# Low parts of the weights on VectorE, layer 1's value tile behind its four u tiles, and new durations in the kernel's own scheduler

## The chip, the cores and the metric

The kernel runs on one core of one Trainium2 chip. The metric is the device time of one execution in microseconds, lower is better. Five engines have instruction streams of their own: TensorE (PE in the profile, its weight loads PEld), VectorE (DVE), ScalarE (ACT), GpSimd (POOL) and SyncE (SP), which issues all DMA transfers. Each engine takes its stream strictly in order, and an instruction waits on semaphores for results of others; what stands behind a waiting instruction waits too.

## What is computed

Two layers of a diffusion backbone over 128 context tokens and 1024 latent tokens, model width 1024. Each layer, cut to what matters here:

```python
h = _rmsnorm(x, norm_w) * (1.0 + scale) + shift      # shift, scale, gate = split(silu(c) @ w_ada + b_ada)
p = h @ w_in                                          # (tokens, 2304): q 512, k 128, v 128, ga 512, u 512, gp 512
q, k = _rope_2d(q), _rope_2d(k)                       # latent tokens only
attn = banded attention, |i-j| <= 128, plus all 128 cached context keys, with a sink logit
pool = (window means of u, windows 2, 4, 8, 16, minus u) @ w_pool * pool_scale
a  = _rmsnorm(attn) * attn_norm * silu(ga);  pl = _rmsnorm(pool) * pool_norm * silu(gp)
x  = x + gate * (concatenate([a, pl]) @ w_out)
```

After the second layer comes one more rmsnorm. All of it is fp32. The new keys and values of the context tokens are outputs too.

## The kernel before

**Tiling.** Activations lie transposed, features on partitions. The 1152 tokens are three groups of 384 columns (group 0: 128 context and 256 latent tokens; buffers `G_81`, `G_82`, `G_83` hold x and later q and the pool result of groups 0, 1, 2). A projection *job* is one tile of 128 output features for one group: `project` issues 24 matmuls of 384 columns into one PSUM buffer `acc`, of which there are two. The 24 are 8 input blocks k times three, since an fp32 value is carried as a high and a low part of type fp32r: `w_hi*h_hi + w_hi*h_lo + w_lo*h_hi`. The parts of h are in `H_78`, `H_79`, `H_80` (groups 0, 1, 2); those of a weight tile in `wh`, of which there are two buffers.

**Weights.** `wload` fetches a weight tile in two halves of 128x512 into `wr` (or into slots of `R`). `wsplit` makes of each half the high part (a cast on ScalarE) and the low part (raw minus high). Which engine subtracts is one line:

```python
eng = self.V_ if i in self.WDVE or second is not None and h == 0 else self.P_
```

`WDVE = (0, 1, 2)` names the first three weight tiles; `second` marks the tiles of the second pass of the output projection, which loads the eight tiles again for group 2. All others are on GpSimd. A `wh` buffer comes free when its tile's last job is done, so the cast of tile n+2 waits for TensorE's last job of tile n.

**Stages of a layer.** 18 tiles times 3 groups are 54 jobs of the input projection, in the order of a list: u0, u1, v, u2, u3, k, q0 to q3, gp0 to gp3, ga0 to ga3; then 24 jobs of the output projection, 16 for groups 0 and 1, then 8 for group 2. With 78 jobs a layer there are 156. Beside them run: `pool_mix` (window sums of the u tiles in the buffer `R` on VectorE, small edge products on GpSimd, matmuls from `pth` and `ptl`), of which u2 and u3 need the buffers of u0 and u1 and after which the cosine and sine tables are loaded over `R` (`R<-in_cs`); the rotation of k and q, which needs these tables; `attention`, 18 units a layer (scores `pst<-K,qs` and `pst<-K,ql`, masked maximum into `s` on VectorE, exponentials on ScalarE, `den` on VectorE, normalisation `s<-s,den` on GpSimd, transposes `pst<-cst,s`, a split into `pth` on ScalarE and `ptl` on VectorE, products `pv<-..,V`); and at the layer's end `zsplit`, which overwrites `H` with the gated branches once the group's last job of the input projection is done. `next_h` then makes layer 1's `H` while the second pass runs.

**What sets the order.** Nothing is scheduled at run time. While the program is built, each stage is a Python generator, and `Sched.run` takes the step with the best priority among those whose estimated time has come; whatever it issues goes to the end of its engine's stream. The clock is TensorE's: `Tensor.issue` moves it on by an estimated cost, and the jobs (`main`, priority 9) fill in, three matmuls at a step, when nothing else is due. `Engine.cost` estimates the other engines, and `ready` adds `LAT` to a result that another engine made. So wrong estimates do not make a wrong result, they make another order. Before, one matmul of 384 columns is reckoned at 384/2.39 = 161 ns, every hand-over between engines at 190 ns, and VectorE and GpSimd as independent.

Of the kernel before, what the change touches and what calls it, by code (L numbers as in the profile page):

```python
# [84 lines left out]
class Engine:  # L85
# [7 lines left out]

    def cost(self, op, n, args, kw):
        if self.name == "act":
            return (205 if "accum_out" in kw else 107) + 0.763 * n
        if self.name == "dve":
            if op == "reciprocal":
                return 70 + 6.6 * n
            if op == "tensor_scalar" and not any(isinstance(x, bass.AP) and x.space == bass.MemoryType.PSUM for x in args):  # L100
                return 70 + 0.52 * n
            return 70 + 1.04 * n
        if op == "tensor_tensor" and kw.get("op") == ALU.pow:
            return 400 + 165 * n
        return 70 + {"tensor_tensor": 2.35, "scalar_tensor_tensor": 1.46}.get(op, 1.2) * n

    def __getattr__(self, op):
        f = getattr(self.eng, op)

        def call(*args, **kw):  # L110
# [6 lines left out]
            self.free = start + self.cost(op, free_size(args[0]), args, kw)  # L117
            s.commit(ins, outs, self.free, self.name)
            s.step_end = max(s.step_end, self.free + s.LAT)
# [4 lines left out]
class Tensor:  # L124
    def __init__(self, sched, eng):
        self.sched, self.eng = sched, eng

    def issue(self, ins, out, c):
        s = self.sched
        start = max(s.clock, s.ready(ins, [out], "pe"))  # L130
        s.stall += start - s.clock
        s.clock = start + c
        s.commit(ins, [out], s.clock + 60, "pe")
        s.step_end = max(s.step_end, s.clock + 60 + s.LAT)

    def matmul(self, out, lhsT, rhs, start, stop):
        self.eng.matmul(out, lhsT, rhs, start=start, stop=stop)  # L137
        n = free_size(rhs)
        if rhs.dtype == R32:
            c = n / 2.39 if n >= 256 else 213  # L140
        elif lhsT.shape[-1] > 32:
            c = max(n * 4 / 2.4, 426)
        else:
            c = n * 4 / 2.4 / 4
        self.issue([lhsT, rhs], out, c)

    def transpose(self, out, in_, ident):
        self.eng.transpose(out, in_, ident)  # L148
        self.issue([in_], out, 109)
# [19 lines left out]
class Sched:  # L169
# [3 lines left out]
    LAT = 190  # L173

    def __init__(self):
# [5 lines left out]
        self.mem = {}  # L181

    def ready(self, ins, outs, eng):
        t = 0.0
        for aps, write in ((ins, False), (outs, True)):
            for ap in aps:
                name, p0, p1, lo, hi = span(ap)
                for (q0, q1, l, h), e in self.mem.get(name, {}).items():
                    if q0 < p1 and p0 < q1 and l < hi and lo < h:
# [3 lines left out]
                        elif eng != "pe":  # L193
                            t = max(t, w)
# [57 lines left out]
class Kernel:  # L252
# [9 lines left out]
    WDVE = (0, 1, 2)  # L262
# [921 lines left out]
    def main(self, order):  # L1184
# [3 lines left out]
        for l in range(DEPTH):  # L1188
# [50 lines left out]
    def run(self):  # L1239
        a = self.a  # L1240
        order = [COL_U, COL_U + 1, COL_V, COL_U + 2, COL_U + 3, COL_K, 0, 1, 2, 3] + [COL_GP + j for j in range(4)] + [COL_GA + j for j in range(4)]
        items = []
        self.order, self.items = order, items
# [66 lines left out]
```

## Time and profile before

| | us |
|---|---|
| median of 3 runs (lowest to highest) | 972.14 (969.76 to 972.52) |
| the profiled execution | 972.32 |
| its span, first to last instruction | 970.5 |
| TensorE matmuls busy | 919.0 (95%) |
| VectorE busy | 710.6 (73%) |
| ScalarE busy | 533.1 (55%) |
| GpSimd busy | 404.2 (42%) |

The span is 1.8 us shorter than the profiled execution's own time. Busy means that at least one instruction of the engine was in progress. In the timeline views a bracket behind a row is the idle time of that engine just before the row and what ended it.

### The profile page before, as it was taken

The numbers are of one execution on the slowest core, as the hardware profiler recorded it, in microseconds if no ns is written. First come the engines' busy times: TensorE is split into PE (matmuls) and PEld (weight loads), VectorE is DVE, ScalarE is ACT, GpSimd is POOL, SyncE is SP. The second block draws the span as 40 slices with busy tenths as digits, with TensorE's granted clock in tenths as the row PEclk, the third lists the DMA queues.
The fourth block names the chain that finished last, engine by engine and source line by source line (L and its number), as shares of the span: only waits on it lengthen the run. The fifth ranks groups of instructions, "written<-read, shape, count | busy, mean of one in ns | idle before, by whom it ended". The sixth has DMA issues, their size and how long they took to land.

```text
span 970.5 us, 15980 instructions
## 1 busy us (share of the span) xinstructions
PE 919.0 (95%) x5576; PEld 853.9 (88%) x5576; DVE 710.6 (73%) x1629; ACT 533.1 (55%) x1279; POOL 404.2 (42%) x419
## 2 busy tenths in 40 slices
PE   6899999999999999999989998999999999899995
PEld 2677787999999998899989998988999999899995
DVE  4876567788887569866797466888897776985675
ACT  3453334457766677653455433446776657875442
POOL 2142246663343354345333323776345326434331
PEclk9999999999999999999999999999999999999998
DMA  9714775010000010335431202000000001213463
GB/s 350 296 55 158 233 252 193 23 39 29 22 23 23 23 32 18 120 112 182 169 125 57 75 25 89 23 33 33 24 22 23 23 23 45 71 49 104 137 201 136
DMA packets 42560, 89.02 MB, mean 92 GB/s; under 512 B 4976, under 2 KB 7664, under 8 KB 42480
## 3 DMA queue, kind: packets, MB, share of 16 engines
q1 hardware_dynamic: 42480, 88.00, 26.4%
q8 instruction: 44, 0.72, 0.3%
q14 instruction: 36, 0.29, 0.1%
HBM read 78.28 MB, written 9.70 MB: 91 GB/s over the span
## 4 chain that ended last, share of the span: by engine, by line
PE 69%; DVE 18%; issue 5%; POOL 3%; ACT 3%; DMA 1%; SPq 0%; POOLq 0%; DVEq 0%; ACTq 0%
PE acc L137 46%; PE pst L137 10%; PE pst L148 7%; PE pv L137 6%; DVE G L111 5%; DVE H L111 3%; DVE t L111 2%; DVE R L111 2%; DVE s L111 2%; ACT s L111 1%; DVE ql L111 1%; DMA G<-in_xT 1%; POOL wh L111 1%; DVE den L111 1%; POOL t L111 1%
## 5 line engine op out<-in xcount | busy, mean ns | idle before, releaser
L137 PE MATMUL acc<-H,wh 128*128 128x384 f32 x3624 | 689.9, 339 | 16.2 <-DVE H L111 9.8
L137 PEld LDWEIGHTS acc<-H,wh 128*128 128x128 f32 x3624 | 633.1, 189 | 42.9 <-DVE H L111 12.2
L111 POOL TENSOR_TENSOR wh<-wr,wh 128x512 fp32r<-128x512 f32 x98 | 134.6, 1386 | 174.3 <-ACT wh L111 165.9
L111 POOL TENSOR_SCALAR s<-s,den 128x512 f32<-128x512 f32 (+2 forms) x144 | 105.3, 746 | 140.3 <-DVE den L111 76.9
L111 DVE TENSOR_TENSOR ptl<-pst,pth 128x512 fp32r<-128x512 f32 x124 | 82.4, 686 | 24.1 <-PE pv L137 14.3
L111 DVE CUSTOM_DVE_ANT_0 s<-pst,cst 128x512 f32<-128x512 f32 (+2 forms) x144 | 84.5, 613 | 13.3 <-PE pst L137 12.7
L111 ACT ACTIVATE s<-s,m 128x512 f32<-128x512 f32 (+2 forms) x144 | 93.9, 655 | 0.6
L111 ACT CAST wh<-wr 128x512 fp32r<-128x512 f32 x100 | 61.0, 616 | 54.9 <-PE acc L137 38.8
L111 ACT CAST pth<-pst 128x512 fp32r<-128x512 f32 x124 | 69.2, 585 | 32.5 <-PE pst L148 21.2
L148 PE MATMUL pst<-cst,s 128*128 128x128 f32 x504 | 70.5, 274 | 6.9 <-POOL s L111 5.3
L148 PEld LDWEIGHTS pst<-cst,s 128*128 128x128 f32 x504 | 59.3, 140 | 14.1 <-POOL s L111 8.9
L137 PE MATMUL pst<-K,ql 128*128 128x256 f32 x272 | 69.2, 283 | 1.0 <-DVE ql L111 0.9
L137 PE MATMUL pst<-K,qs 128*128 128x256 f32 x272 | 69.2, 283 | 0.0
L111 ACT ACTIVATE t<-G 128x384 f32<-128x384 f32 x86 | 43.7, 520 | 44.0 <-DVE G L111 28.1
L111 DVE TENSOR_TENSOR R<-R 128x384 f32<-128x384 f32 (+13 forms) x60 | 43.3, 722 | 25.9 <-ACT R L111 24.5
L111 ACT CAST qs<-G 64x256 fp32r<-64x256 f32 x144 | 58.2, 404 | 2.6
L111 DVE SCALAR_TENSOR_TENSOR G<-acc,mods,G 128x384 f32<-128x384 f32 (+2 forms) x64 | 31.5, 512 | 33.8 <-PE acc L137 33.5
L137 PEld LDWEIGHTS pst<-K,ql 128*128 128x128 f32 x272 | 51.3, 189 | 3.4 <-DVE ql L111 1.8
L137 PEld LDWEIGHTS pst<-K,qs 128*128 128x128 f32 x272 | 51.4, 189 | 0.3
L137 PE MATMUL pv<-ptl,V 128*128 128x512 f32 x124 | 50.2, 419 | 0.0
L111 POOL TENSOR_TENSOR rr<-rr,nhalf 128x3 f32<-128x3 f32 x21 | 21.5, 1026 | 68.6 <-DVE rr L111 68.3
L111 ACT COPY t<-pv 64x256 f32<-64x256 f32 x72 | 23.2, 369 | 47.0 <-PE pv L137 46.2
(125 smaller groups left out, 1206.2 us busy)
## 6 DMA issues: line engine op xcount, KB each, us to landing
wr<-in_wi SPq DMA_DIRECT2D x68, 256.0 KB, 2.6
s<-in_wada SPq DMA_DIRECT2D x44, 256.0 KB, 4.3
wr<-in_wo SPq DMA_DIRECT2D x32, 256.0 KB, 2.7
R<-in_wo SPq DMA_DIRECT2D x32, 256.0 KB, 3.8
wk<-in_wada SPq DMA_DIRECT2D x12, 512.0 KB, 7.8
G<-in_xT SPq DMA_DIRECT2D x6, 768.0 KB, 9.5
G<-in_xT SPq DMA_DIRECT2D x12, 384.0 KB, 3.9
xs<-G SPq DMA_DIRECT2D x12, 384.0 KB, 2.4
```

The costliest lines, as they stand in the source:

```text
L111: r = f(*args, **kw)
L137: self.eng.matmul(out, lhsT, rhs, start=start, stop=stop)
L148: self.eng.transpose(out, in_, ident)
```

## The change

Three things, and no other:

- `WDVE` becomes `range(200)`, so VectorE makes the low parts of all weight tiles. GpSimd made 98 halves out of `wr` and 16 out of `R`.
- Layer 1 gets a list of its own: u0, u1, u2, u3, v, then as before. Layer 0 keeps v between u1 and u2.
- The scheduler's estimates are new: costs by engine, operation and whether an operand is in PSUM; a `TAIL` per engine until the result is there; `LAT` 40 in place of 190; 384/2.4 + 13 = 173 ns for a matmul of 384 columns; a price for TensorE to go over between matmuls, transposes and 32-column matmuls; and `port`, by which an instruction of GpSimd and one of VectorE that touches no PSUM are not started beside each other.

```diff
+    TAIL = dict(act=105, dve=82, pool=45)
+    HOLD = dict(dve=50, pool=95)
     def cost(self, op, n, args, kw):
...
-            return (205 if "accum_out" in kw else 107) + 0.763 * n
-        if self.name == "dve":
+            c = 280 + 0.83 * n if "accum_out" in kw else (80 + 0.755 * n if psum else 73 + 0.855 * n) + 100 * column
+        elif self.name == "dve":
...
-            return 70 + 1.04 * n
-        if op == "tensor_tensor" and kw.get("op") == ALU.pow:
-            return 400 + 165 * n
-        return 70 + {"tensor_tensor": 2.35, "scalar_tensor_tensor": 1.46}.get(op, 1.2) * n
+                c = 65 + 1.05 * n + (62 if column and op == "scalar_tensor_tensor" else 0)
+        elif kw.get("op") == ALU.pow:
+            c = 360 + 165 * n
+        elif op == "tensor_tensor":
+            c = 138 + 2.165 * n
+        else:
+            c = 225 + 0.865 * n
+        return c, self.name == "pool" or self.name == "dve" and not psum and op != "memset"
...
-            self.free = start + self.cost(op, free_size(args[0]), args, kw)
-            s.commit(ins, outs, self.free, self.name)
+            c, port = self.cost(op, free_size(args[0]), args, kw)
+            if port:
+                start = max([start] + [t for n, t in s.port.items() if n != self.name])
+                s.port[self.name] = start + c + self.TAIL[self.name] - self.HOLD[self.name] - 85
+            self.free = start + c
+            end = self.free + self.TAIL[self.name]
+            s.commit(ins, outs, end, self.name)
...
-    def issue(self, ins, out, c):
+    DRAIN = 165
+
+    def issue(self, ins, out, c, mode="mm"):
         s = self.sched
-        start = max(s.clock, s.ready(ins, [out], "pe"))
+        start = max(s.clock, s.ready(ins, [out], "pe") - 60)
         s.stall += start - s.clock
-        s.clock = start + c
-        s.commit(ins, [out], s.clock + 60, "pe")
+        if mode != self.mode:
+            if self.mode == "col":
+                start = max([start] + list(self.cols.values()))
+            start += 110 if "col" in (mode, self.mode) else 85 if self.mode == "tr" else 0
+            self.mode, self.cols = mode, {}
...
-            c = n / 2.39 if n >= 256 else 213
+            self.issue([lhsT, rhs], out, max(n / 2.4 + 13, 109))
...
-    LAT = 190
+    LAT = 40
...
-    WDVE = (0, 1, 2)
+    WDVE = range(200)
...
-        order = [COL_U, COL_U + 1, COL_V, COL_U + 2, COL_U + 3, COL_K, 0, 1, 2, 3] + [COL_GP + j for j in range(4)] + [COL_GA + j for j in range(4)]
+        last = [COL_K, 0, 1, 2, 3] + [COL_GP + j for j in range(4)] + [COL_GA + j for j in range(4)]
+        u = [COL_U + j for j in range(4)]
+        orders = [u[:2] + [COL_V] + u[2:] + last, u + [COL_V] + last]
```

`main` and `run` take the list of their layer. The instructions are the same in kind and number, but for the engine of the 114 subtractions; their order changes on every engine. In the changed file the helpers' lines are L128 (was L111), L172 (L137) and L180 (L148). Three places:

ScalarE in layer 1, around the jobs of k. `t<-acc` takes a job's result out of its `acc` buffer, 128x256 and 128x128 for group 0 and 128x384 for groups 1 and 2; `K<-t` stores the rotated keys; `wh<-wr` is the high part of a weight half. Before:

```order
L111 CAST wh<-wr 128x512
L111 CAST K<-t 64x384 x2
L111 COPY t<-acc 128x384
L111 CAST wh<-wr 128x512
L111 CAST K<-t 64x384 x2
L111 COPY t<-acc 128x384
```

and now:

```order
L128 CAST K<-t 64x384 x2
L128 COPY t<-acc 128x384
L128 CAST wh<-wr 128x512 x2
L128 CAST K<-t 64x384 x2
L128 COPY t<-acc 128x384
```

The first of the two casts stood ahead of the copy of k's group 1; now both stand behind it.

TensorE at the first attention unit of layer 1, from the last of its scores to the first transposes of its weights `s`. Before:

```order
L137 MATMUL pst<-K,ql_85 128x256
L137 MATMUL acc<-H_80,wh 128x384 x15
L137 MATMUL acc<-H_78,wh 128x384 x9
L148 MATMUL pst<-cst,pre 128x128 x3
L137 MATMUL acc<-H_78,wh 128x384 x15
L137 MATMUL acc<-H_79,wh 128x384 x3
L148 MATMUL pst<-cst,s 128x128 x4
```

and now:

```order
L172 MATMUL pst<-K,ql_85 128x256
L172 MATMUL acc<-H_78,wh 128x384 x12
L180 MATMUL pst<-cst,pre 128x128 x3
L172 MATMUL acc<-H_78,wh 128x384 x12
L172 MATMUL acc<-H_79,wh 128x384 x24
L172 MATMUL acc<-H_80,wh 128x384 x6
L180 MATMUL pst<-cst,rr 128x128 x3
L172 MATMUL acc<-H_80,wh 128x384 x9
L180 MATMUL pst<-cst,s 128x128 x4
```

Between the two stand 42 job matmuls before and 63 now.

VectorE at the end of the second pass of layer 0. `G_83<-acc` closes a job of group 2, `H_79` is made for the second job of layer 1, and `R 128x8` (a memset) belongs to the first job of layer 1. Before:

```order
L111 SCALAR_TENSOR_TENSOR G_82<-G_82,hs_74,s 128x384 x2
L111 SCALAR_TENSOR_TENSOR G_83<-acc,mods_71,G_83 128x384
L111 SCALAR_TENSOR_TENSOR H_79<-G_82,mods_72,H_79 128x384 x3
L111 TENSOR_TENSOR R<-R,t 128x384
L111 SCALAR_TENSOR_TENSOR G_83<-acc,mods_71,G_83 128x384
```

and now:

```order
L128 SCALAR_TENSOR_TENSOR G_83<-acc,mods_71,G_83 128x384
L128 SCALAR_TENSOR_TENSOR G_82<-G_82,hs_74,s 128x384 x3
L128 TENSOR_TENSOR wh<-wr,wh 128x512
L128 TENSOR_TENSOR R<-R,t 128x384
L128 TENSOR_TENSOR wh<-wr,wh 128x512
L128 SCALAR_TENSOR_TENSOR H_79<-G_82,mods_72,H_79 128x384
L128 MEMSET R 128x8
```

All eight of `H_79` stood ahead of the last `G_83<-acc`; now five of the eight stand behind it.

## Rows read from the trace of the kernel before

**Rows 1.** The head of the page: the span, and of each engine busy us, share of the span and instructions.

```profile
span 970.5 us, 15980 instructions
PE 919.0 (95%) x5576; PEld 853.9 (88%) x5576; DVE 710.6 (73%) x1629; ACT 533.1 (55%) x1279; POOL 404.2 (42%) x419
```

**Rows 2.** Busy time by stretch: from and to, length, busy us (and instructions) of PE, PEld, DVE, ACT and POOL, granted TensorE clock, DMA share and GB/s.

```profile
0.00:70.00 70.00, 55.40 (x374) 37.49 (x375) 46.23 (x118) 34.84 (x76) 20.52 (x23) 1.00 0.62 236
...
225.00:365.00 140.00, 139.80 (x893) 134.42 (x891) 106.45 (x278) 95.64 (x239) 56.22 (x62) 1.00 0.08 27
365.00:400.00 35.00, 31.19 (x193) 29.12 (x192) 33.73 (x78) 25.76 (x65) 15.64 (x15) 1.00 0.20 63
...
480.00:517.00 37.00, 33.31 (x186) 31.21 (x186) 33.95 (x63) 19.86 (x43) 14.29 (x10) 1.00 0.45 152
...
565.00:612.00 47.00, 41.38 (x221) 39.46 (x221) 32.91 (x58) 17.27 (x39) 17.25 (x19) 0.96 0.17 59
612.00:645.00 33.00, 31.02 (x180) 29.99 (x179) 27.70 (x62) 15.40 (x42) 24.15 (x24) 0.95 0.10 33
...
820.00:855.00 35.00, 31.30 (x195) 29.30 (x193) 33.78 (x77) 26.37 (x66) 15.76 (x15) 1.00 0.20 66
```

**Rows 3.** Who waited for whom, the row of TensorE's waits for the normalised weights `s`: us in total, times, longest us.

```profile
PE pst L148 <- POOL s L111: 5.3, 11, 1.7
```

**Rows 4.** One row of the chain of work that ended last, in the first pass of the output projection of layer 0: start, us, what.

```profile
435.91 32.27 PE acc L137 x186
```

**Rows 5.** Timeline of layer 1 at the jobs of k and the first of q, over all engines: start, us, engine, instruction, shapes, count.

```profile
580.45 4.16 DVE L111 TENSOR_TENSOR R<-R 128x398 f32<-128x398 f32 x4 [1.33 <-ACT R L111]
...
585.13 0.45 PE L137 MATMUL pst<-ptl,s 128*128 128x384 f32 x1 [0.94 <-DVE ptl L111]
...
592.67 0.43 DVE L111 TENSOR_TENSOR t<-t,R 128x256 f32<-128x256 f32 x1 [2.15 <-DMA R<-in_cs]
...
595.09 0.62 ACT L111 CAST wh<-wr 128x512 fp32r<-128x512 f32 x1 [3.11 <-PE acc L137]
...
596.67 0.48 ACT L111 COPY t<-acc 128x384 f32<-128x384 f32 x1
...
597.20 6.00 PE L137 MATMUL acc<-H,wh 128*128 128x384 f32 x24 [2.19 <-ACT t L111]
...
608.71 3.59 PE L137 MATMUL acc<-H,wh 128*128 128x384 f32 x19 [0.82 <-ACT G L111]
```

**Rows 6.** Busy time as in rows 2, in the two stretches where the granted clock falls inside the kernel.

```profile
595.00:603.00 8.00, 5.81 (x25) 5.68 (x24) 5.07 (x8) 3.76 (x8) 4.19 (x3) 0.79 0.19 66
633.00:641.00 8.00, 6.26 (x30) 5.81 (x30) 5.52 (x13) 2.53 (x6) 5.53 (x7) 0.79 0.19 68
```

**Rows 7.** Timeline around the first adds of window 8 in layer 1 (GpSimd, VectorE, TensorE).

```profile
564.38 2.86 POOL L111 TENSOR_TENSOR wh<-wr,wh 128x512 fp32r<-128x512 f32 x2 [2.01 <-ACT wh L111]
564.72 3.53 DVE L111 TENSOR_TENSOR R<-R 128x390 f32<-128x390 f32 x3 [1.68 <-ACT R L111]
...
568.77 0.45 PE L137 MATMUL pst<-ptl,s 128*128 128x384 f32 x1 [1.35 <-DVE ptl L111]
...
569.22 1.75 DVE L111 TENSOR_TENSOR R<-R 128x390 f32<-128x390 f32 x3
```

**Rows 8.** Timeline of the first attention unit of layer 1, whose last score matmul starts at 624.90.

```profile
634.15 0.94 POOL L111 TENSOR_SCALAR s<-s,den 128x128 f32<-128x128 f32 x2 [0.39 <-DVE rr L111]
634.80 0.68 PE L148 MATMUL pst<-cst,s 128*128 128x128 f32 x2 [1.72 <-POOL s L111]
```

**Rows 9.** Timeline of TensorE and VectorE where the input projection of layer 0 goes over into the output projection.

```profile
383.24 1.14 PE L137 MATMUL acc<-H,wh 128*128 128x384 f32 x5 [1.66 <-DVE H L111]
...
388.89 1.66 PE L137 MATMUL acc<-H,wh 128*128 128x384 f32 x8 [0.90 <-DVE H L111]
```

**Rows 10.** Timeline of TensorE in the second pass of layer 0 (waits for the low part of a weight, and for the sum of squares before layer 1).

```profile
487.87 4.08 PE L137 MATMUL acc<-H,wh 128*128 128x384 f32 x22 [0.77 <-POOL wh L111]
...
503.34 7.21 PE L137 MATMUL acc<-H,wh 128*128 128x384 f32 x40 [1.03 <-POOL wh L111]
...
511.70 0.52 PE L148 MATMUL pst<-cst,R 128*128 128x128 f32 x3 [1.15 <-DVE R L111]
```

**Rows 11.** Groups of instructions by line, engine, operation and shape: count, busy us, mean ns of one, idle us before them and what ended it.

```profile
L111 POOL TENSOR_TENSOR wh<-wr,wh 128x512 fp32r<-128x512 f32 x98 | 134.6, 1386 | 174.3 <-ACT wh L111 165.9 <-PE pst L137 4.7 <-DVE R L111 3.1
L111 POOL TENSOR_TENSOR wh<-R,wh 128x512 fp32r<-128x512 f32 x16 | 22.5, 1404 | 45.7 <-ACT wh L111 38.7 <-DVE G L111 7.0
L111 DVE TENSOR_TENSOR wh<-R,wh 128x512 fp32r<-128x512 f32 x16 | 11.5, 720 | 0.6
L111 DVE TENSOR_TENSOR H<-G,H 128x384 fp32r<-128x384 f32 x52 | 33.7, 683 | 1.0 <-POOL G L111 1.0
```

**Rows 12.** Instructions by the tile they write: duration ns minimum/median/maximum, first and last start.

```profile
L111 DVE TENSOR_TENSOR H<-G,H x52: 535/550/1648, 67.3 to 906.7; 128x384 fp32r<-128x384 f32 x52
L111 DVE TENSOR_TENSOR ptl<-pst,pth x124: 670/686/693, 183.3 to 879.3; 128x512 fp32r<-128x512 f32 x124
```

**Rows 13.** The low and high parts alone (tile `wh`) by stretch; columns as in rows 2, so the fifth busy column is GpSimd's subtractions.

```profile
365.00:400.00 35.00, 21.44 (x111) 19.30 (x111) 0.00 (x0) 2.47 (x4) 4.50 (x4) 1.00 0.20 63
480.00:517.00 37.00, 32.95 (x180) 30.60 (x180) 3.94 (x5) 7.60 (x13) 13.44 (x9) 1.00 0.45 152
```

**Rows 14.** Who waited for whom, the row on the high parts: us in total, times, longest us.

```profile
ACT wh L111 <- PE acc L137: 63.9, 28, 4.7
```

More of the change, by code (lines that the diff above doesn't have):

```diff
@@ L116, in call @@
             start = max(self.free, s.clock, s.ready(ins, outs, self.name))
-            self.free = start + self.cost(op, free_size(args[0]), args, kw)
-            s.commit(ins, outs, self.free, self.name)
-            s.step_end = max(s.step_end, self.free + s.LAT)
+            c, port = self.cost(op, free_size(args[0]), args, kw)
[5 more added lines that the diff above has]
+            s.commit(ins, outs, end, self.name)
+            s.step_end = max(s.step_end, end + s.LAT)
             return r
@@ L126, in __init__ @@
         self.sched, self.eng = sched, eng
-    def issue(self, ins, out, c):
+        self.mode, self.cols = "mm", {}
+    DRAIN = 165
+    def issue(self, ins, out, c, mode="mm"):
         s = self.sched
-        start = max(s.clock, s.ready(ins, [out], "pe"))
+        start = max(s.clock, s.ready(ins, [out], "pe") - 60)
         s.stall += start - s.clock
-        s.clock = start + c
-        s.commit(ins, [out], s.clock + 60, "pe")
-        s.step_end = max(s.step_end, s.clock + 60 + s.LAT)
+        if mode != self.mode:
[3 more added lines that the diff above has]
+            self.mode, self.cols = mode, {}
+        if mode == "col":
+            p = span(out)[1]
+            end = max(start, self.cols.get(p, 0.0)) + c
+            self.cols[p], s.clock = end, start + 35
+        else:
+            end = s.clock = start + c
+        s.commit(ins, [out], end + self.DRAIN, "pe")
+        s.step_end = max(s.step_end, end + self.DRAIN + s.LAT)
     def matmul(self, out, lhsT, rhs, start, stop):
@@ L139, in matmul @@
         if rhs.dtype == R32:
[L140 to L145 removed]
+            self.issue([lhsT, rhs], out, max(n / 2.4 + 13, 109))
+        else:
+            self.issue([lhsT, rhs], out, n * 4 / 2.4, "col")
     def transpose(self, out, in_, ident):
         self.eng.transpose(out, in_, ident)
[L149 removed]
+        self.issue([in_], out, 109, "tr")
 class Queue:
@@ L181, in __init__ @@
         self.mem = {}
+        self.port = {}
     def ready(self, ins, outs, eng):
@@ L1182, in job, with main @@
         self.flag("job", l, c, g)
-    def main(self, order):
+    def main(self, orders):
         sc = self.sc
@@ L1187, in main @@
         self.left = {}
-        for l in range(DEPTH):
+        for l, order in enumerate(orders):
             pos = {c: i + n for n, c in enumerate(order)}
@@ L1253, in run @@
         sc.spawn(self.wsplit(items), 0)
-        sc.spawn(self.main(order), 9)
+        sc.spawn(self.main(orders), 9)
         sc.run()
```

22 lines of the change are left out of this document (16 added, 6 removed).

## The prediction

> **What bounds the kernel now.** The page's busy times come first: TensorE is busy 919.0 of 970.5 us, the next engine, VectorE, 710.6 [rows 1]. So 51.5 us of the span have no matmul, and only there, or where the clock is low, can a change of order save time, for the matmuls stay what they are. The chain of waits gives their pace where nothing is late: 186 in 32.27 us, 173.5 ns each, so a job of 24 takes 4.16 us [rows 4]. The stretches then show where the idle time lies [rows 2]. In the middle of the attention of layer 0 TensorE idles 0.20 of 140 us: nothing can be won there, only lost. It idles in the first 70 us (14.6), at the two ends of an input projection (3.8 and 3.7), in the second pass of layer 0 (3.7) and at the start of layer 1 (5.6 and 2.0). In two stretches there the granted clock is 0.79 on average over 8 us [rows 6]; with the two levels 1.2 and 2.4 GHz that is 3.4 us each at the lower one, which costs some 1.7 us each.
>
> The sum below is made against the profiled execution, 972.32 us, which stands 1.8 over its own span and 0.2 over the median of the runs.
>
> **A. Layer 1's order, and ScalarE around k.** TensorE waits 2.19 us at 597.20 for a copy that empties `acc`, and 0.82 us at 608.71 for another [rows 5]. The rows before say why: the cosine table lands only at 592.67, since the window sums of u3 run until then; and the copy of k's group 1 (596.67) stands in ScalarE's stream behind the high part of a weight, which itself waited until 595.09 for TensorE's last job on the old buffer. TensorE's next job needs the copy, so it waits for a queue that waits for it. The change removes both: with v behind u3 the window sums have three jobs more, 12.5 us, and both casts now stand behind that copy. The idle 3.0 us go, and with the long gap the low clock behind it, 1.7: 4.7 us. The order shows this directly; I take 4.5.
>
> **B. VectorE held up by GpSimd's subtractions.** Three adds take 3.53 us beside two subtractions on GpSimd, and 1.75 when GpSimd has none; TensorE then waits 1.35 us for what follows them [rows 7]. Four adds take 4.16 us, and 0.94 us are lost again [rows 5]. This is 2.3 us in layer 1. With the 114 subtractions gone from GpSimd, that cause goes, but VectorE now spends their time itself, earlier or later in the same queue: I take 1.5.
>
> **C. Normalised weights.** TensorE waits 5.3 us in 11 places for GpSimd's `s` [rows 3], 1.72 of them at layer 1's first unit [rows 8], where the second low-clock stretch follows [rows 6]: 7.0 us with its 1.7. Two things help. GpSimd loses 134.6 + 22.5 = 157.1 of its 404.2 us [rows 1, 11]. And the order now puts 63 job matmuls between the scores and the transposes, 10.9 us, where 42, 7.3 us, stood; the chain took from 624.90 to 635.09, 10.2 us [rows 8], so this wait should vanish. Part of the rest belongs to D. I take 4.0 of the 7.0.
>
> **D. The ends of the input projections.** Here VectorE is the bound: 33.73 of 35 us [rows 2], and TensorE waits 1.66 and 0.90 us for `H` [rows 9]; layer 1's end idles as much [rows 2]. On the one hand the four subtractions that GpSimd does there [rows 13] add 4 x 0.69 = 2.8 us to VectorE. On the other hand the new order ends attention one to two jobs earlier, so less of it falls into these 35 us, and puts attention's transposes and scores between the last jobs of the projection, where before TensorE ran through bare jobs and arrived early. Bounds: all 7.5 us go, or VectorE overflows by 33.73 + 2.8 - 35 = 1.5 us twice, a loss of 3. The order speaks for the gain, and the gain is limited by the load; I take 4.5.
>
> **E. Second pass of layer 0.** TensorE waits 0.77 and 1.03 us for GpSimd's low part and 1.15 for the sum of squares [rows 10]. On VectorE a low part takes 0.72 instead of 1.40 us [rows 11], and the transposes of the sum of squares now stand a quarter job later. But nine subtractions [rows 13] add 6.2 us to VectorE's 33.95 of 37 [rows 2], and five of eight `H_79` now stand behind the last output job; the second job of layer 1 would wait about 1 us for the last of them. Of 3.0 us, I take 2.0.
>
> **F. Start and end.** DMA order is unchanged in the first 60 us, and the first three tiles' low parts were VectorE's before. I take nothing of the first 70 us, with 2 us either way, and nothing at the tail, which is one chain after the last job.
>
> **G. What it costs elsewhere.** VectorE gets 114 x 0.69 = 78.7 us. Some comes back: `H<-G,H` takes 535 ns at best but 683 on average, 52 x 0.148 = 7.7 us in this group alone, and only operations on two SBUF operands are held up so: `ptl<-pst` from PSUM stays between 670 and 693 [rows 11, 12]. I leave the other groups open. At 106.45 of 140 us in attention [rows 2], VectorE has room. The price is slack. The old scheduler reckoned 161 ns for matmuls of 173.5 and 190 ns for each hand-over, so data were early; the new one is close to the truth, and half of what is close comes late. Bounds: nothing, or in each of the 36 attention units one wait like the mean one for `s`, 5.3/11 = 0.48 us [rows 3], 17 us. Job matmuls fill in three at a time, 0.52 us, and cover most of it, so I stay near the low end: 5 us.
>
> The Trainium skill (SBUF — State Buffer, section SBUF: two separate sides) says that VectorE and GpSimd share a pair of SBUF ports as an exclusive lock, held for the whole instruction, against VectorE operations with two SBUF inputs. The trace agrees: 1648 ns at worst for `H<-G,H`, 693 for the PSUM-fed `ptl`. By it, a subtraction on VectorE can itself be held by what is left on GpSimd; with the 720 ns that it takes there already [rows 11], G's first figure would be 82.1 instead of 78.7.
>
> **Sum.** 4.5 + 1.5 + 4.0 + 4.5 + 2.0 = 16.5 saved, 5 given back: 972.3 - 11.5 = 960.8. I say 961.
>
> **Rivals.**
>
> *R1, the slack is needed.* G comes at its upper end, 17: 972.3 - 16.5 + 17 = 973, no change. For it: attention idles only 0.20 us of 140 now [rows 2], so every new wait shows. Against it: waits of two lanes overlap, and new distances such as C's are longer than the chain. Chance 0.13.
>
> *R2, VectorE becomes the bound (slower).* At D and E the load overflows: 1.5 + 1.5 + (33.95 + 6.2 - 37 = 3.2) = 6.2 us. And each low part now waits in VectorE's stream for its high part, which waits for TensorE to free the buffer, 28 times and 63.9 us before [rows 14]; where scores or `ptl` stand behind it, TensorE waits in turn. At 0.48 us for each of the 28 that is 13.4. A and half of C come all the same, 6.5; B, D and E do not: 972.3 + 6.2 + 13.4 - 6.5 = 985. It decides once the relief from GpSimd is under the 6.2 us at those places. Against it: there the order shows less of attention, and low parts standing right behind their casts. The Trainium skill (Perfetto Trace Analysis, section Optimizing Scalar/DVE Operations) advises to move work off VectorE, even to GpSimd, where VectorE is saturated, and adds that the shared port may undo it. That rule speaks for R2 at D, where the rows show 96%. Chance 0.13.
>
> *R3, layer 1's start does not mend.* The casts or the table are late all the same: A gives nothing and C 2. 972.3 - 10 + 5 = 967. Chance 0.14.
>
> *R4, all of it.* A to E in full, 4.7 + 2.3 + 7.0 + 7.5 + 3.0 = 24.5, and G nothing: 948. Chance 0.10.
>
> **How the numbers follow.** The forecast, 953 to 966, has 0.50. About 0.3%, 2.9 us, is what a measurement of this kernel can tell from no change, so the line is at 969.2 and 975.0. Faster: 0.50, R4's 0.10, 0.11 of R3 and 0.02 of R1, 0.73. Slower: 0.12 of R2 and 0.02 of R1, 0.14. The same: 0.13. The range leaves out R2 and the outer half of R4: 948 to 975.
>
> **What would show it.** A right: no wait of TensorE over 0.5 us among the jobs of k and q, and a clock of 1.00 from 565 to 645. B: three adds of window 8 in 1.75 us. C: waits on `s` under 2 us. D: under 2.5 us idle at each end. E: no wait for `wh`, one of about 1 us for `H` in layer 1's second job. G: 3 to 8 us idle in the attention stretches that now idle 0.20; VectorE 740 to 780 us busy. The prediction is wrong if the attention stretches idle 15 us, or if TensorE waits for `H` at the ends of the projections longer than now.

## The result and the profile after

The changed kernel takes 947.08 us (median of 4 runs, 946.33 to 947.95) against 971.55 for the kernel before in the same comparison: a ratio of 0.975, 95% interval 0.9732 to 0.9769. The profiled execution took 946.36 us, 26.0 less than the profiled one of before. The forecast was 961, its range 948 to 975, so the time lies just outside, at the rival "all of it".

The head of the page and TensorE's row, to be set against [rows 1]:

```profile
span 944.6 us, 16049 instructions
PE 912.7 (97%) x5576; PEld 851.5 (90%) x5576; DVE 731.9 (77%) x1743; ACT 533.1 (56%) x1279; POOL 250.2 (26%) x305
```

GpSimd lost 154.0 us, where 157.1 were reckoned. VectorE got 114 subtractions more and is only 21.3 us busier. Busy time by stretch, columns and stretches as in [rows 2]. The stretches are the same times, not the same work: the changed kernel runs 3.6 us ahead near 365 us and 28.6 near 690. The table of jobs further down compares the same work.

```profile
0.00:70.00 70.00, 57.13 (x393) 40.13 (x394) 51.04 (x127) 35.96 (x79) 20.49 (x26) 0.98 0.64 239
225.00:365.00 140.00, 139.87 (x893) 132.81 (x891) 121.18 (x316) 100.91 (x253) 42.98 (x53) 1.00 0.06 20
365.00:400.00 35.00, 33.97 (x210) 32.88 (x211) 33.31 (x88) 28.32 (x73) 8.47 (x11) 1.00 0.27 84
480.00:517.00 37.00, 35.20 (x202) 34.13 (x201) 33.52 (x75) 20.94 (x45) 2.78 (x4) 1.00 0.26 87
565.00:612.00 47.00, 45.27 (x267) 44.16 (x267) 36.12 (x69) 21.73 (x49) 28.11 (x24) 1.00 0.15 49
612.00:645.00 33.00, 33.00 (x201) 32.84 (x200) 29.21 (x77) 14.55 (x43) 15.66 (x18) 1.00 0.14 47
820.00:855.00 35.00, 34.51 (x206) 32.62 (x205) 29.21 (x69) 24.95 (x61) 6.00 (x8) 1.00 0.31 102
```

In 365 to 400 VectorE is busy 33.31 of 35 us, hardly less than the 33.73 of before, and yet TensorE's idle time falls from 3.8 to 1.0. The clock is 1.00 through layer 1's start. The waits of TensorE that answer to [rows 3, 5, 9] (us in total, times, longest), first for `H` before, then all of after:

```profile
PE acc L137 <- DVE H L111: 9.8, 7, 2.2
```

```profile
PE pst L180 <- POOL rr L128: 3.2, 3, 1.8
...
PE acc L172 <- DVE H L128: 1.6, 2, 0.8
...
PE acc L172 <- ACT G L128: 1.3, 1, 1.3
...
PE pst L180 <- POOL s L128: 0.8, 2, 0.6
...
PE acc L172 <- ACT t L128: 0.2, 1, 0.2
```

`s` fell from 5.3 to 0.8 us and `H` from 9.8 to 1.6; of the 3.2 for `rr`, 1.8 is at the kernel's tail, as before. VectorE's groups, to be set against [rows 11], and the same group `R<-R,t` of before:

```profile
L128 DVE TENSOR_TENSOR wh<-wr,wh 128x512 fp32r<-128x512 f32 x100 | 73.7, 746 | 24.3 <-ACT wh L128 21.2 <-PE pst L172 2.0
L128 DVE TENSOR_TENSOR wh<-R,wh 128x512 fp32r<-128x512 f32 x32 | 21.1, 687 | 0.5
L128 DVE TENSOR_TENSOR H<-G,H 128x384 fp32r<-128x384 f32 x52 | 28.7, 574 | 0.1
L128 DVE TENSOR_TENSOR R<-R,t 128x384 f32<-128x384 f32 x42 | 23.5, 560 | 6.3 <-ACT t L128 6.1
```

```profile
L111 DVE TENSOR_TENSOR R<-R,t 128x384 f32<-128x384 f32 x42 | 31.6, 752 | 12.2 <-ACT t L111 12.2
```

And the sum `den` by tile, as in [rows 12], of after and then of before:

```profile
L128 DVE TENSOR_TENSOR den<-den,es x72: 139/160/694, 179.3 to 838.6; 128x2 f32<-128x2 f32 x72
```

```profile
L111 DVE TENSOR_TENSOR den<-den,es x72: 142/160/1293, 176.3 to 870.3; 128x2 f32<-128x2 f32 x72
```

An add of two columns, 0.16 us at the median, took up to 1.29 us before. The moved work is 98/100 x 73.7 + (21.1 - 11.5) = 81.8 us; VectorE rose by 21.3; so 60.5 us of its old busy time are gone. Busy time counts the overlap of successive instructions once. By the sum of VectorE's durations, 780.1 us before and 814.0 after, 83.7 us of moved work cost 33.9, so instructions got shorter by 49.8 us, 7.7 of which the prediction had counted. What they had been waiting for is the question of the experiments.

**Where the 25.9 us of the span came from.** The table is worked out from the traces: for the stretch between the starts of two job matmuls (24 to a job, numbered through both layers; layer 1 starts at job 78; the first stretch begins with the span and the last ends with it), its length less the time that its TensorE instructions take back to back (reckoned at columns/2.4 + 13 ns for a matmul, 173 ns for 384 columns, at 109 ns for a transpose, and at columns/4.8 ns for each of the 304 32-column matmuls). That work is 878.1 us in every kernel here; what is left is lost time, in us. w, o and s are the three parts of the change (low parts, order, scheduler), alone and together; wos is the whole.

```
jobs        0-8   8-32  32-52 52-56 56-72 72-80 80-88 88-112 112-132 132-136 136-156
before     29.90 12.55  2.21  5.00  0.67  5.49  0.19  17.15   2.13    5.00   12.13
w          27.43 16.32  5.04  0.27  0.24  0.10  0.19  10.73   3.21    0.33   11.76
o          30.17 12.89  2.25  5.34  0.60  5.48  0.18   4.37   6.55    2.47   12.17
s          25.06 14.17  5.25  5.50  0.84  7.26  0.17   9.99   4.12    6.94   12.63
wo         29.84 16.27  5.01  0.24  0.28  0.14  0.15   7.00   5.04    0.15   12.12
os         25.23 11.52  5.31  3.95  1.11  7.26  0.17   6.72   4.91    2.86   12.77
ws         23.82  9.86  4.15  1.32  0.77  2.81  0.47   9.08   4.85    3.60   12.90
wos        24.37 10.28  4.08  1.32  0.80  2.80  0.15   3.81   4.62    1.59   12.66
wos-port   30.15 16.66  4.89  1.30  0.67  0.61  0.15   7.72   4.21    1.33   12.92
wos+sub    24.62 21.32  4.65  3.17  4.29 11.30  1.27   8.68   7.57    4.42   13.67
wos+pow    23.83 13.60  4.14  1.66  1.49  2.76  0.15   3.75   4.85    1.67   12.73
wos lat190 25.70 17.13  2.79  8.43  0.50  3.07  0.15   2.04   4.99   13.79   12.10
wos mix30  24.01 10.34  4.35  1.21  0.81  2.02  0.15   3.03   1.85    0.21   12.00
```

From before to wos: layer 1's start (jobs 88 to 112) -13.3; the ends of the input projections (52 to 56, 132 to 136) -7.1; the first jobs (0 to 8) -5.5; the second pass of layer 0 (72 to 80) -2.7; jobs 8 to 32 -2.3; the middle of attention (32 to 52, 112 to 132) +4.4; the rest +0.6. Sum -25.9.

Each row is one execution, and the lost time holds what a low clock costs. In before 3.4 of the 17.15 us are clock [rows 6]. In w the mean clock is 0.72 from 138 to 150 us, around waits of 1.02 and 2.17 us: two levels as in [rows 6] make that 3.4 of its 16.32 us. In wo it is 0.89 from 45 to 60 us and 0.91 from 60 to 80, which is 3.4 of its 29.84; w issues its first jobs in the same order, has 1.00 there, and loses 2.4 less. So two or three us in one stretch of one row can be the clock alone.

### The profile page after: what moved, and what is told of

Its sections match the earlier page's. It is cut to its first block, busy times and chain, and to the rows that moved or that the text cites. A ratio compares the mean times of both kernels' runs of the same rounds, so it can differ in the third digit from the quotient of the medians.

```text
span 944.6 us, 16049 instructions
## 1 busy us (share of the span) xinstructions
PE 912.7 (97%) x5576; PEld 851.5 (90%) x5576; DVE 731.9 (77%) x1743; ACT 533.1 (56%) x1279; POOL 250.2 (26%) x305
## 4 chain that ended last, share of the span: by engine, by line
PE 82%; ACT 5%; issue 5%; DVE 4%; POOL 2%; DMA 1%; SPq 0%; POOLq 0%; DVEq 0%; ACTq 0%
PE acc L172 57%; PE pst L172 11%; PE pst L180 7%; PE pv L172 7%; DVE G L128 2%; ACT s L128 2%; ACT qs L128 1%; ACT wh L128 1%; POOL rr L128 1%; ACT pth L128 1%; ACT t L128 1%; DMA R<-in_cs 1%; POOL pre L128 1%; DVE wh L128 1%; DMA G<-in_xT 1%
## 5 line engine op out<-in xcount | busy, mean ns | idle before, releaser
L172 PE MATMUL acc<-H,wh 128*128 128x384 f32 x3624 | 683.9, 338 | 4.1 <-DVE H L128 1.6
L172 PEld LDWEIGHTS acc<-H,wh 128*128 128x128 f32 x3624 | 631.1, 188 | 25.4 <-issue 8.6
L128 POOL TENSOR_SCALAR s<-s,den 128x512 f32<-128x512 f32 (+2 forms) x144 | 104.7, 740 | 250.0 <-DVE den L128 100.6
L128 ACT CAST pth<-pst 128x512 fp32r<-128x512 f32 x124 | 69.3, 583 | 46.6 <-PE pst L180 41.5
L128 ACT ACTIVATE s<-s,m 128x512 f32<-128x512 f32 (+2 forms) x144 | 94.1, 656 | 1.6 <-DVE m L128 1.0
L128 ACT CAST wh<-wr 128x512 fp32r<-128x512 f32 x100 | 61.1, 618 | 59.5 <-PE acc L172 55.3
L128 DVE TENSOR_TENSOR ptl<-pst,pth 128x512 fp32r<-128x512 f32 x124 | 83.3, 685 | 13.8 <-ACT pth L128 10.8
L128 DVE CUSTOM_DVE_ANT_0 s<-pst,cst 128x512 f32<-128x512 f32 (+2 forms) x144 | 83.9, 611 | 12.8 <-PE pst L172 11.0
L128 DVE TENSOR_TENSOR wh<-wr,wh 128x512 fp32r<-128x512 f32 x100 | 73.7, 746 | 24.3 <-ACT wh L128 21.2
L128 POOL TENSOR_TENSOR rr<-rr,nhalf 128x3 f32<-128x3 f32 x21 | 20.9, 995 | 229.1 <-DVE rr L128 228.1
L128 ACT ACTIVATE t<-G 128x384 f32<-128x384 f32 x86 | 43.9, 521 | 44.3 <-DVE G L128 26.1
L172 PE MATMUL pst<-K,qs 128*128 128x256 f32 x272 | 68.4, 283 | 0.4 <-ACT qs L128 0.2
L172 PE MATMUL pst<-K,ql 128*128 128x256 f32 x272 | 67.9, 281 | 0.0
L180 PE MATMUL pst<-cst,s 128*128 128x128 f32 x504 | 66.6, 273 | 0.9 <-POOL s L128 0.8
L180 PEld LDWEIGHTS pst<-cst,s 128*128 128x128 f32 x504 | 58.7, 140 | 4.9 <-POOL s L128 1.6
L128 DVE SCALAR_TENSOR_TENSOR G<-acc,mods,G 128x384 f32<-128x384 f32 (+2 forms) x64 | 31.6, 514 | 40.7 <-PE acc L172 40.6
L128 ACT CAST qs<-G 64x256 fp32r<-64x256 f32 x144 | 58.2, 404 | 2.7
L128 POOL TENSOR_TENSOR G<-G,rb 128x384 f32<-128x384 f32 x40 | 46.3, 1185 | 24.5 <-ACT rb L128 24.5
L172 PEld LDWEIGHTS pst<-K,qs 128*128 128x128 f32 x272 | 51.4, 189 | 1.3 <-ACT qs L128 0.6
L172 PEld LDWEIGHTS pst<-K,ql 128*128 128x128 f32 x272 | 51.3, 189 | 1.2
L172 PE MATMUL pv<-pth,V 128*128 128x512 f32 x124 | 48.8, 420 | 1.9 <-ACT pth L128 1.8
L172 PE MATMUL pv<-ptl,V 128*128 128x512 f32 x124 | 49.6, 408 | 0.0
```

Source lines behind the costliest of these rows:

```text
L128: r = f(*args, **kw)
```

## The experiments

**The three parts alone and in pairs.** Low parts (w): `WDVE`, below. Order (o): layer 1's list. Scheduler (s): the rest of the diff. In this order: w, o, s, wo, os, ws.

```diff
-    WDVE = (0, 1, 2)
+    WDVE = range(200)
```

> The kernel before, with the low parts of all weights on VectorE and nothing else changed (old planner, old order of layer 1). Theory 'planner' (most of the 25 us come from the planner's new estimates): this part alone clears only what GpSimd's subtractions cause directly, the adds of layer 1 (1.5) and the low parts of the second pass (2); jobs 4 to 8 still lose some 5 us and the two ends of the input projections some 5 each: 968 to 971 us. Theory 'GpSimd freed' (most comes from the 157 us taken from GpSimd, since VectorE is then held up less): 957 to 961 us, with the waits for s under 2 us and the ends of the projections under 3 us each.

> The kernel before, with v behind all u in layer 1 and nothing else changed. Both theories: layer 0 keeps its times to within 1 us; in layer 1 the wait of 2.19 us at k and the low clock behind it go, 3.5 to 5 us in jobs 96 to 104; 967 to 969 us. If layer 1's start was held by something else, the wait moves to another job and the time stays at 971 to 973.

> The kernel before, with the new planner and nothing else changed (GpSimd keeps its 114 subtractions, layer 1 its old order). Theory 'planner': jobs 4 to 8 lose under 1.5 us instead of 5.5, the ends of the projections under 2.5 each instead of 5.0, the waits for s under 2 us: 953 to 959 us. Theory 'GpSimd freed': the planner alone only moves the same waits about, and gives back slack: 966 to 974 us.

> The kernel before with the low parts on VectorE and the new order of layer 1, but the old planner. The two alone gave 16.6 and 10.6 us. Theory 'apart' (they mend different waits): 944 to 948 us, and then the new planner adds nothing or costs to the changed kernel's 947. Theory 'shared' (both clear layer 1's start, some 8 us of it the same): 952 to 955 us, and the planner is worth 5 to 8 on top of them.

> The changed kernel with GpSimd's 114 subtractions put back (new planner, new order of layer 1). Theory 'GpSimd freed': the planner knows the subtractions but can't hide them beside s and the window sums; 14 to 18 us slower than the changed kernel, 961 to 965 us. Theory 'the planner's port does the same work': it keeps the two engines apart by itself, 950 to 955 us.

> The changed kernel with layer 1's old order (new planner, low parts on VectorE). Theory 'apart': the order is worth as much here as alone, 8 to 11 us: 955 to 958 us, lost between jobs 88 and 112. Theory 'shared': with the subtractions gone and the plan that knows the durations, layer 1's start runs through in either order: 947 to 951 us.

| parts | median us | ratio to before | 95% interval |
|---|---|---|---|
| w | 956.33 | 0.9827 | 0.9814 to 0.9840 |
| o | 962.32 | 0.9889 | 0.9875 to 0.9903 |
| s | 969.03 | 0.9960 | 0.9948 to 0.9972 |
| wo | 954.55 | 0.9819 | 0.9806 to 0.9833 |
| os | 961.74 | 0.9898 | 0.9884 to 0.9911 |
| ws | 956.71 | 0.9836 | 0.9818 to 0.9854 |
| wos | 947.08 | 0.9750 | 0.9732 to 0.9769 |

Theory "GpSimd freed" holds for w in its time (0.7 us under the range) and at the ends of the projections (0.3 each), but `s` still waits 3.9 us, where it expected under 2. Theory "planner" falls for s alone. The order gains 10.8 us (1.1% of 972), more than either theory gave it. For wo "shared" holds, for os "GpSimd freed", for ws "apart". The parts don't add up: alone they give 1.7, 1.1 and 0.4%, 3.2 in all, together 2.5. Taken off the whole, w costs 0.9898 - 0.9750 = 1.5%, o 0.9%, s 0.7%. The table tells where they overlap: w and o each clear layer 1's start in part (17.15 to 10.73 and 4.37), and wo is no better there than o. w alone clears the ends of the projections and the second pass (15.5 us to 0.7), and s takes 5.0 of that back. But w with the old planner loses 3.8 more in jobs 8 to 32, 3.4 of it clock, and nearly 4 more in the middle of attention. The profiled s stands 2.8 us over its median, the profiled ws 3.2 under; their rows in the table are to be read with that.

The wait at the end of k is a clean case. TensorE's waits for `t`, of w, of s and of ws (the three without the new order):

```profile
PE acc L137 <- ACT t L111: 4.8, 3, 2.1
```

```profile
PE acc L172 <- ACT t L128: 5.4, 3, 2.2
```

```profile
PE acc L172 <- ACT t L128: 3.3, 3, 2.1
```

The longest, 2.1 to 2.2 us, is in each that of [rows 5] at the end of k. With the new order it is gone (0.2 in wos).

**What the move of the low parts buys: port or queue.** Two kernels keep the order of the changed one and give GpSimd 114 instructions more, which nothing reads and of which the planner knows nothing: the old subtractions, or powers on six columns.

```diff
+                if not (i < 3 or second is not None and h == 0):
+                    self.nc.gpsimd.tensor_tensor(self.scr, raw, parts[0][h].bitcast(F32), op=ALU.subtract)
```

```diff
+                if not (i < 3 or second is not None and h == 0):
+                    self.nc.gpsimd.tensor_tensor(self.scr[:, 0, 0:6], parts[0][h][:, 0, 0:6].bitcast(F32), self.ones[:, 0:6], op=ALU.pow)
```

> The changed kernel; in addition GpSimd does its 114 old subtractions into a scratch tile that nobody reads, unknown to the planner, so the order of all other work is that of the changed kernel. This gives GpSimd back its 157 us. Theory 'freed' (what the move of the low parts buys is VectorE and GpSimd's other work going through unheld, not an earlier low part): 10 to 16 us slower than the changed kernel, 957 to 963 us. Rival 'the low parts came late': GpSimd's work beside them hurts little, 947 to 951 us.

> As the run with scratch subtractions, but each is replaced by a power on 128x6, about as long on GpSimd (360 + 165 x 6 = 1350 ns by the planner's numbers) and, by the rows of the kernel before, without holding up VectorE (beside 128x3 powers `ql` takes its 420 ns). Theory 'held port': GpSimd's queue is as busy, yet the time stays within 3 us of the changed kernel: 945 to 950 us. Theory 'GpSimd's queue': s, rr and pre stand behind the extra work and come late, 957 to 963 us, as with the subtractions.

The subtractions: 984.56 us, ratio 1.0129 (1.0116 to 1.0142), 37 us over the changed kernel. The powers: 949.12 us, 0.9769 (0.9756 to 0.9781), 2 over it, at the edge of what can be told. Theory "freed" holds in kind, but the subtractions cost more than twice the 10 to 16 us that it expected; theory "held port" holds. Head of the page, and GpSimd's and VectorE's groups, first with subtractions:

```profile
PE 926.1 (94%) x5576; PEld 851.8 (87%) x5576; DVE 820.8 (83%) x1743; ACT 534.9 (54%) x1279; POOL 428.8 (44%) x419
...
L429 POOL TENSOR_TENSOR scr<-wr,wh 128x512 f32<-128x512 f32 x98 | 154.2, 1573 | 111.0 <-ACT wh L128 86.6 <-issue 11.9 <-ACT es L128 10.0
L128 DVE TENSOR_TENSOR wh<-wr,wh 128x512 fp32r<-128x512 f32 x100 | 99.5, 1003 | 19.1 <-ACT wh L128 18.2
```

and with powers:

```profile
PE 915.1 (96%) x5576; PEld 853.1 (90%) x5576; DVE 729.7 (77%) x1743; ACT 533.5 (56%) x1279; POOL 422.5 (45%) x419
...
L429 POOL TENSOR_TENSOR scr<-wh,ones 128x6 f32<-128x6 f32 x114 | 177.2, 1554 | 148.2 <-ACT wh L128 131.0 <-ACT es L128 14.5
L128 DVE TENSOR_TENSOR wh<-wr,wh 128x512 fp32r<-128x512 f32 x100 | 72.7, 736 | 25.9 <-ACT wh L128 22.7 <-PE pst L172 2.0
```

GpSimd is as busy in both, by instructions of nearly the same length. Only the subtractions hold VectorE: 820.8 busy us against 729.7, for the same work. So what the move buys is the end of the collisions of VectorE's work with GpSimd's two-operand subtractions, hardly GpSimd's queue. The two kernels differ in one thing more: the subtractions read `wr`, so SyncE waits for them with new loads, 100.0 us in 68 places. Little of that reaches the other engines: ScalarE's casts wait 6.2 us for `wr`, 3.1 in the changed kernel.

The Trainium skill (SBUF — State Buffer, section SBUF: two separate sides) calls this an exclusive lock, held for the whole instruction, between VectorE operations with two SBUF inputs and GpSimd operations that read SBUF. The subtractions agree: the low part on VectorE goes from 736 to 1003 ns. The powers do not: they too read SBUF, for 1554 ns each, and VectorE's 729.7 us show nothing of it. Here the measurement decides, and no pair of runs separates the other kinds of GpSimd operations.

These kernels show the price of holding VectorE in a plan that doesn't expect it; where the planner knows of the subtractions (os), they cost 0.9898 - 0.9750, 14.4 us.

**What the planner's parts do.** wos-port takes the lines on `port` out; the second run puts a like rule into wo's old planner; the third is the changed kernel with `LAT` 190.

```diff
-            if port:
-                start = max([start] + [t for n, t in s.port.items() if n != self.name])
-                s.port[self.name] = start + c + self.TAIL[self.name] - self.HOLD[self.name] - 85
```

```diff
+            if self.name == "pool" or self.name == "dve" and not psum and op != "memset":
+                start = max([start] + [t for n, t in s.port.items() if n != self.name])
+                s.port[self.name] = start + c - 50
```

> The changed kernel, with the planner's port taken out (its other estimates stay). Theory 'port': it is the port in the plan that puts GpSimd's s and VectorE's SBUF work apart and 10.9 us of work between scores and transposes, where the plan now leaves 7.0 at the first unit of each layer; TensorE waits for s some 5 us again, and VectorE's sum of durations rises by 10 us or more: 952 to 958 us. Theory 'durations': the costs and hand-overs do it, and the port adds nothing: 945 to 949 us.

> Low parts on VectorE and the new order of layer 1, with the old planner's costs and hand-overs and only the port added to it. Theory 'port' (what the planner buys is that SBUF work of the two engines is kept apart; the durations buy nothing): 941 to 948 us. Theory 'durations' (the port works only with costs close to the truth): 952 to 957 us, as without the port.

> The changed kernel with the planner's hand-over time put back from 40 to 190 ns, its other estimates as changed. Theory 'slack' (what the changed kernel loses in the middle of attention, 4 to 5 us in each layer against 2, is planned too tightly): 2 to 5 us less there in all, 941 to 945 us. Rival (those waits come from VectorE's load and stay, and a longer lead only moves work): 946 to 952 us.

Without the port 959.22 us (0.9860, 0.9847 to 0.9873), later than expected and 0.4% over wo: the new durations without the port cost some 4 us. Old durations with the port: 979.7 (1.0071, 1.0057 to 1.0086). New ones with 190 ns: 970.08 (0.9981, 0.9969 to 0.9992). Theory "port" holds for the changed kernel, though not in all its signs: `s` waits 3.9 us, not 5, the sum of VectorE's durations rises by 3.5 us, not 10, and the table puts the loss in jobs 0 to 32 (12.2 us) and 88 to 112 (3.9). For the old durations both theories fall; that kernel's trace loses 19.1 us in jobs 52 to 56, where wo loses 0.2, and why its plan breaks there stays open. With 190 ns theory "slack" falls, and its rival's range is missed by 18 us as well. In the table, lat190 gains 1.3 in the middle of layer 0 and loses 19.3 at the ends of the projections (its last scores stand 56.4 and 57.5 jobs into their layer, 55.6 and 55.9 in the changed kernel).

**How sharp the planner's values are.** `DRAIN` 175 for 165, `LAT` 20 and 60 for 40.

> The changed kernel with TensorE's drain in the planner at 175 instead of 165 ns. The order then differs from the changed kernel's in a few places alone (39 lines of difference on TensorE). Theory 'truth': within 1 us of the changed kernel, 946 to 948. Rival 'chance of the plan': even so small a step moves the time by 2 us or more, up or down.

> The changed kernel with 20 instead of 40 ns for a hand-over in the planner. Here the last scores of attention stand 54.9 and 54.75 jobs into their layer, where the changed kernel has them at 55.6 and 55.9. Theory 'where attention ends': the two ends of the input projections lose under 1 us each instead of 1.3 and 1.6, and the second pass no more than now: 943 to 946 us. Theory 'truth' (tighter than the truth is late everywhere): 948 to 953 us.

> The changed kernel with 60 instead of 40 ns for a hand-over. The last scores stand at 56.5 and 55.4 jobs. Theory 'where attention ends': layer 0's end loses 3 to 6 us more, layer 1's the same as now: 950 to 953 us. Theory 'truth, in proportion': an eighth or so of what 190 ns cost (23 us over 150 ns), 3 us: 949 to 951 us.

948.05 us (0.9741, 0.9724 to 0.9759), 952.46 (0.9800, 0.9786 to 0.9813) and 947.54 (0.9750, 0.9737 to 0.9764). The first and third are the changed kernel's time; 20 ns is 5 us slower, in the range of theory "truth", and 60 ns costs nothing, where both theories expected 3 or more. (Layer 0's end does lose 4.2 us more there, as expected; other stretches give it back.) So neither theory holds for both: no slope that leads to the truth, and where attention ends doesn't tell the time either. Plans next to each other differ by up to 5 us.

**Old and new estimates in one plan.** From job 30 (or 36) of each layer to its end the old costs, 190 ns and no port hold.

```diff
+                sc.LAT = 190 if 30 <= n + (6 if l == 0 else 0) < 99 else 40
```

> The changed kernel, but from job 30 of each layer to the layer's end the planner reckons with the old estimates (costs, 190 ns, no port); low parts and order of layer 1 as changed. If the stretches can be had apart: jobs 0 to 32 lose 35 us as in the changed kernel, the ends of the projections and the second pass some 2 us in all instead of 5.7: 942 to 945 us. If a plan is one piece (attention here ends at 56.3 and 57.0 jobs, not at 52.4 as with the old planner throughout, so the ends are crowded again): 948 to 956 us.

> The same with the change of estimates at job 36 of each layer; the last scores stand at 57.1 and 54.9 jobs. Apart: 942 to 945 us. One piece: layer 0's end loses 4 to 8 us, layer 1's 1 to 3: 947 to 954 us.

Job 30: 940.19 us, 0.9668 (0.9652 to 0.9683), faster than both kernels. Job 36: 952.61, 0.9795 (0.9779 to 0.9810), slower than the changed one. The stretches can be had apart in the first (before job 32 it loses what wos loses, in jobs 112 to 136 2.1 in place of 6.2; the time is 2 us under the range), not in the second, where layer 0's end loses 5.2 us, as "one piece" expected. A good plan among neighbours, then, not a rule. Its stretch 365 to 400, and that of w:

```profile
365.00:400.00 35.00, 34.47 (x216) 32.52 (x215) 34.25 (x92) 27.99 (x70) 6.71 (x10) 1.00 0.28 83
```

```profile
365.00:400.00 35.00, 34.66 (x210) 32.38 (x209) 31.07 (x85) 27.64 (x73) 7.93 (x12) 1.00 0.10 27
```

VectorE is busy 34.25 of 35 us in the first, and yet TensorE idles only 0.5.

## Why the prediction was wrong, step by step

The direction held, and so did most of the causes; two steps of the sum failed. The first is what was taken off A to E, above all off C (4.0 of 7.0) and D (4.5 of 7.5, "the gain is limited by the load"): in full they were 24.5, the prediction took 16.5, and the stretches that hold their waits gave 13.3 + 7.1 + 2.7 + 2.3 = 25.4. The second is **F**, "I take nothing of the first 70 us", which gave 5.5. With G's 4.4 + 0.6 given back as reckoned (5), 960.8 - 8.9 - 5.5 = 946.4, the profiled time.

- **A: right in mechanism, mis-sized.** The order alone is worth 10.8 us, not 4.5, since it clears more than A's waits. In o the adds of B run unheld too (three of window 8 in 1.76 us), the waits behind them are gone, and so is C's 1.72 at layer 1's first unit; the longest wait left there is 0.9. So A, B and that part of C are not separate terms. The sum took the named waits; the stretch from job 88 to 112 had 17.15 us to lose, waits under half a microsecond among them, and the order alone leaves 4.37 (it loses 4.4 again in jobs 112 to 132 and gains 2.5 at layer 1's end). One expected sign was wrong: a wait of 1.28 us remains at q's first tile. Timeline of the changed kernel there:

```profile
578.80 1.23 POOL L128 TENSOR_TENSOR rr<-rr,nhalf 128x3 f32<-128x3 f32 x1
...
579.91 0.56 DVE L128 TENSOR_TENSOR t<-t 128x384 f32<-128x384 f32 x1
...
580.77 8.08 PE L172 MATMUL acc<-H,wh 128*128 128x384 f32 x45
...
585.39 2.62 POOL L128 TENSOR_TENSOR G<-G,rb 128x384 f32<-128x384 f32 x2
...
587.07 1.36 DVE L128 TENSOR_TENSOR t<-t 128x384 f32<-128x384 f32 x1
...
588.46 1.04 ACT L128 CAST K<-t 64x384 fp32r<-64x384 f32 x2 [3.90 <-DVE t L128]
...
590.12 3.42 PE L172 MATMUL acc<-H,wh 128*128 128x384 f32 x18 [1.28 <-ACT G L128]
```

  The add for `t` takes 0.56 us where GpSimd ends a power and then rests, and 1.36 beside its product; `K<-t` waits for it, and the copy that empties `acc` stands behind `K<-t`. By the durations it is the same cause that the change took away elsewhere; no run tried it at this place.

- **B: right in mechanism.** Low parts and order each do it alone. Three adds of window 8 take the time that [rows 7] gave for GpSimd silent:

```profile
545.73 1.76 DVE L128 TENSOR_TENSOR R<-R 128x390 f32<-128x390 f32 x3
```

- **C: mis-sized, and one of its two reasons counts for little.** `s` waits 0.8 us in all, under the 2 expected, and its low clock is gone: 4.5 + 1.7 = 6.2 us, where 4.0 was taken. The reason "GpSimd loses 157.1" alone leaves 3.9 us of waits (w), the order of layer 1 alone 3.8 (o), the planner alone 2.6 (s); and with the powers back on GpSimd, which is then 422.5 us busy, they are 1.7. At layer 1's first unit GpSimd ends `s` at 618.76 (617.35 + 1.41) and TensorE comes for it at 620.84, without a wait:

```profile
617.35 1.41 POOL L128 TENSOR_SCALAR s<-s,den 128x128 f32<-128x128 f32 x4
...
620.84 0.60 PE L180 MATMUL pst<-cst,s 128*128 128x128 f32 x4
```

- **D: the step that failed in its reason, too.** "Here VectorE is the bound: 33.73 of 35 us": a busy time was read as a load, and 4.5 was taken where 7.1 came. Part of that busy time was VectorE being held by GpSimd's subtractions, so adding four of them to VectorE and taking them from GpSimd relieves it. w alone brings both ends from 5.0 to 0.3, but it doesn't prove this: its attention also ends earlier (last scores 52.4 and 53.3 jobs into their layer, 56.9 and 57.0 before), as the prediction's other reason has it. The pair with one order does: wos+sub loses 3.2 and 4.4 at the two ends, where wos loses 1.3 and 1.6. TensorE waits for `H` at neither end any more. The 1.3 and 1.6 that remain in the changed kernel come with the new planner (s: 5.5 and 6.9), and the 3 us of overflow never came.

- **E: near (2.7 for 2.0), but as a difference that the prediction didn't see.** No wait for `wh` is left, and one of 0.75 us for `H` in layer 1's second job, as expected. w alone gains all but 0.1 of the 5.5; with the new planner 2.8 are lost again, the wait for `H` among them.

- **F: wrong.** Its reason doesn't reach: the loads of the first 38 us and the first low parts stay as they were (two small loads that stood at 50 us, of the cache and of `w_pool`, now stand at 62), but the planner orders TensorE's first jobs anew. Before, TensorE waited 2.18 us for `H` at 47.13, group 2's first job started before its `H` was there and then stood, and later the window sums came late. Timeline of before:

```profile
47.13 0.62 PE L137 MATMUL acc<-H,wh 128*128 128x384 f32 x2 [2.18 <-DVE H L111]
...
65.54 0.62 PE L137 MATMUL acc<-H,wh 128*128 128x384 f32 x2 [1.14 <-DVE H L111]
...
72.95 2.73 POOL L111 TENSOR_TENSOR wh<-wr,wh 128x512 fp32r<-128x512 f32 x2
73.16 2.81 DVE L111 SCALAR_TENSOR_TENSOR t<-R 128x128 f32<-128x128 f32 x2
76.56 0.44 PE L137 MATMUL pst<-pth,s 128*128 128x384 f32 x1 [1.02 <-ACT pth L111]
```

  and of the changed kernel:

```profile
63.62 0.69 PE L172 MATMUL acc<-H,wh 128*128 128x384 f32 x3
...
64.65 8.12 PE L172 MATMUL acc<-H,wh 128*128 128x384 f32 x45
...
69.91 0.62 DVE L128 SCALAR_TENSOR_TENSOR t<-R 128x128 f32<-128x128 f32 x2
```

  s alone gives 4.8 of it, w alone 2.5, and without the port 30.15 is lost again, with waits of 1.15, 0.94 and 0.99 us for `H`: the planner that knows of the port places this work so that `H` is ready. The two `t<-R` at 73.16 are once more VectorE beside two subtractions.

- **G: the size right, the reasons not.** The middle of attention loses 4.4 us more, but not as idle time in the stretch named (0.13 of 140), and VectorE is 731.9 busy, not 740 to 780. "The price is slack" is not borne out: w with the old, generous estimates loses 3.9 more there as well, and 190 ns put back gains 0.9. What makes these 4.4 us stays open.

- **The rivals.** R1 and R2 fell with G's and D's reasons; R2's point, that relief from GpSimd is under 6.2 us at those places, is answered by the changed kernel: 7.1 at the ends and 2.7 in the second pass, 9.8 together. R3 fell with A. R4's 948 came so near by luck: it has nothing for F and nothing for G, and F's 5.5 happened to make up for what G gave back. The advice cited from the Trainium skill (Perfetto Trace Analysis, section Optimizing Scalar/DVE Operations), work off a saturated VectorE even to GpSimd, would here have been the wrong way; its own warning of the shared port is what the runs show.

The planner's 6.7 us (0.9819 to 0.9750) are shown as a sum, and so is that the port in it is needed (10.7 us with it out). Why its parts do harm one by one, and why one plan is 5 us better than its neighbour was not settled.

## What to carry to other kernels

Before an engine's busy share is read as load, compare the same instruction's median and longest times: `den`'s 0.16 and 1.29 us said that VectorE was waiting. Moving two-operand work from GpSimd to VectorE can then pay even where VectorE shows 96%; what counts is the sum of durations unheld. When named waits are summed, sum the whole stretch's loss as well: the small ones were 6.8 of 17.2 us here (4.7, 2.3 and 3.4 were named), and they went with the rest. And a list scheduler's estimates are to be tried as plans, several of them, since 20 ns in one of them moved the time by 5 us here.

## What the runs showed of the hardware

- GpSimd powers on 128x6 run 1.55 us each and leave VectorE alone (729.7 busy us against 731.9 without them); subtractions on 128x512 of 1.57 us, in the same places of the same order, cost VectorE 91 us.
- A small instruction of VectorE is held as a large one is: an add on 128x2 took up to 1.29 us.
- Both sides pay: when each engine makes the same difference, GpSimd's subtraction takes 1573 ns, where it took 1386 before [rows 11], and VectorE's 1003 in place of 736.
